# One token-row fetch a pass, VectorE in written order, and another order of passes and of last norms in a mixture-of-experts decoder layer

## The chip, the cores and the metric

One NeuronCore of a Trainium2 chip runs the whole layer. The metric is the device time of one execution in microseconds (us). A time is the median of three executions; the profile is of one more execution of the same program.

## The reference

The input is 512 tokens of 1024 float32 numbers. The layer projects them, runs four mLSTM heads and eight sliding-window attention heads side by side, adds the result to the input and normalises. Then comes a mixture of 32 experts, of which each token uses two, and a second normalisation:

```python
def hierarchical_moe(...):
    g_idx = argmax(xt @ w_group_router + b)          # one of 4 groups
    top_v, top_i = top_k(e_logits of that group, 2)  # two of its 8 experts
    ...
    for e in range(N_EXPERTS):                        # D_EXPERT = 256
        h = silu(xt @ w_exp_gate[e]) * (xt @ w_exp_up[e])
        out = out + combine[:, e:e + 1] * (h @ w_exp_down[e])
...
x = layer_norm(ALPHA * x + hierarchical_moe(x), ln2_w, ln2_b)
```

Everything that the change touches lies in the mixture of experts and in the last normalisation.

## The kernel before

**Passes.** Once the tokens have been routed, the kernel works in 13 passes, numbered p = 0 to 12. A pass holds 128 seats for tokens, shared out among experts by the letter that `ORDER` gives it: A is one expert with 96 seats and one with 32, B is two experts with 64 seats each, C is four experts with 32 seats each. An expert has 3 MB of weights, so an A or B pass needs 6 MB and a C pass 12 MB. In `"BBBCABABACBBC"` the C passes are 3, 9 and 12.

**What a pass does.** `pairs_x` (L1019) collects the tokens of two passes at a time by products of one-hot tiles (`ohr`, written by VectorE in `hot`, L1012 and L1014) with the token rows `x1h` and `x1l`; `pick_out` (L1025, L1027) copies the result to `xs`. `gu_part` (L1106) is gate and up, one half of the weights after the other; `pair_h` makes the hidden vector (ScalarE L1119, VectorE L1120); `dn_t` transposes it (TensorE L1127, VectorE copy to `ht`, L1129); `dn_mm` (L1137) is down. TensorE's order is written out: gate and up of pass p with the transpose of pass p-1 in its middle, then, for odd p, the collection of the next two passes, then down of pass p-1.

**What becomes of a pass's result.** For p below `KEPT` = 8, `y_store` writes the weighted rows to `yd` in HBM. For later passes `y_split` (L1147 on ScalarE, L1148 on VectorE) cuts them in two parts, `back_hot` (L1173, VectorE) writes a one-hot tile, and `add_back` adds them into the token rows `x1`: eight pairs of products on TensorE (L1185), each followed by a VectorE add (L1186), through two PSUM banks. For the stored rows, `y_gather` fetches each of the four chunks of 128 tokens twice by an indirect DMA on GpSimd's queue (memset L1162, DMA L1163) and VectorE adds them to `x1` (L1166). It is called in passes 8 (chunks 0 and 1) and 9 (chunks 2 and 3).

**Orders and queues.** SyncE's queue carries the weights in a written order (L596 gate and up, L602 and L604 down). They go into a ring of 16 slots of 1 MB (7 + 5 + 4); `release` gives back a pass's gate and up slots and the down slots of the pass before it, `prefetch` issues as many loads as slots have been given back, and each waits on the queue until the last reader of its slot is done. Activations share 16 slots of 4 KB a partition (`mix`): the eight tiles `x1h` and `x1l` hold half of them until the last collection; `xs`, `ohr`, `y`, `yh`, `yl`, `oh2` and `yg` share the rest. A block under `manual_schedule` keeps the written order on the engines that it names; the other engines' order comes from a planner with its own costs. In the pass loop only TensorE (and SyncE) were so named.

**The end.** After the loop a block with the four compute engines in written order does down of pass 11, its `add_back`, and pass 12. A token's final row is normalised by `norm_s` (statistics on VectorE L1618, a short chain on GpSimd), `norm_z` (ScalarE L1630, times `ln2_w` L1631) and `norm_o` (plus `ln2_b` L1636, DMA out L1637). Tokens that have a seat in pass 12 are normalised once more: `base_rows` (L1657, L1659) collects their rows into the PSUM tiles `zr`, the result of pass 12 is added there, and the rows are scattered out (L1707). In VectorE's written order the multiplication of pass 12's hidden vector (L1120) stands behind `norm_z` of chunk 3.

Of the kernel before, what the change touches and what calls it, by code (L numbers as in the profile page):

```python
# [10 lines left out]
F32 = mybir.dt.float32  # L11
F32R = mybir.dt.float32r
# [4 lines left out]
AF = mybir.ActivationFunctionType  # L17
OP = mybir.AluOpType
AX = mybir.AxisListType
ENG = mybir.EngineType  # L20

T = 512
DM = 1024
NCH = 4
P = 128
# [2 lines left out]
DE = 256  # L28
CAP = 64

ORDER = "BBBCABABACBBC"
NP = len(ORDER)
STATIC = 6
NOVER = 32
# [13 lines left out]
KEPT = 8  # L48
# [30 lines left out]
def layer_kernel(ctx, tc, x, w_in, conv_w, conv_b, gate_bias, norm_w, sinks, w_out, ln1_w, ln1_b,  # L79
# [20 lines left out]
    def slot(name, dt=F32, pool=None):  # L100
        _, p_, n = pools[pool or ("front" if name in FRONT else "mix")]
        return p_.tile([P, n], dt, tag="s", name=name)
# [85 lines left out]
    def split(hi, lo, src, eng=V):  # L188
        A.activation(hi, src, AF.Copy)  # L189
        eng.tensor_tensor(lo, src, hi, op=OP.subtract)  # L190
# [887 lines left out]
    def ready(p):  # L1078
        return fetch(p) if p in GATHER else hots(p)
# [75 lines left out]
        G.dma_start(yd[p * P:(p + 1) * P], y)  # L1155


    def y_gather(cs):
        for c in cs:
            for k in range(2):  # L1160
                t = slot("yg")[:, :DM]
                G.memset(t, 0.0)  # L1162
                G.indirect_dma_start(out=t, out_offset=None, in_=yd[:, :],  # L1163
                                     in_offset=bass.IndirectOffsetOnAxis(ap=yrow[:, 2 * c + k:2 * c + k + 1], axis=0),
                                     bounds_check=KEPT * P - 1, oob_is_err=False)
                V.tensor_add(x1[c], x1[c], t)  # L1166

    def y_slots():
        return [slot(n, F32R)[:, :DM] for n in ("yh", "yl")]
# [410 lines left out]
    def back(p):  # L1580
        return back_hot(slot("oh2", F32R)[:, 0:T], toks(p))

    with tc.manual_schedule(engines={ENG.PE}):
        for p in range(2, NP - 1):
            release(p, False)
            if p > 2:
                release(p - 1, True)
            prefetch(99)
            hts = []
            pg = pg2 if p == 2 else pass_gu(xs, p % 2, p, (lambda: hts.append(dn_t(prev))) if prev else None)  # L1590
            h = pair_h(pg)
            if p % 2:
                ob, xs = hn, taken(p + 1, hn)
                if p + 3 < NP:
                    hn = ready(p + 3)
            if prev:
                py = pass_dn(hts[0], p - 1)
                if p - 1 < KEPT:
                    y_store(py, p - 1)
                else:  # L1600
                    y = y_split(py, cws[:, p - 1:p], *y_slots())
                    if p == NP - 2:
                        ht = dn_t(h)
                    add_back(back(p - 1), y)
                if p - KEPT in (0, 1):
                    y_gather(range(2 * (p - KEPT), 2 * (p - KEPT) + 2))
            prev = h
        l2d = l2_parts()
        o = back(NP - 2)
        sm = same_rows(NP - 1)  # L1610

    HS = [slice(0, 512), slice(512, 1024)]
    mvs = {}
# [9 lines left out]

    zo = {}

    def norm_z(c):
        z = zo[c] = slot("z")[:, :DM]
        mv = mvs[c]
        for h, hs in enumerate(HS):
            A.activation(z[:, hs], x1[c][:, hs], AF.Identity, bias=mv[:, 3:4], scale=mv[:, 2:3])  # L1630
            (G if ('VV', 'VG', 'VV', 'GV')[c][h] == "G" else V).tensor_mul(z[:, hs], z[:, hs], l2[0][:, hs])  # L1631

    def norm_o(c):
        z = zo.pop(c)
        for h, hs in enumerate(HS):
            (G if ('VV', 'VV', 'GV', 'GV')[c][h] == "G" else V).tensor_add(z[:, hs], z[:, hs], l2[1][:, hs])  # L1636
        SP.dma_start(o2[c * P:(c + 1) * P], z)  # L1637

    def base(c):
        return [x1[c][:, hs] for hs in HS]  # L1640
# [3 lines left out]
    prefetch(99)  # L1644
    with tc.manual_schedule(engines=MAN):
        zr = [bank("zr", tag=t) for t in ("t", "m")]
        fin = {}

        def x1_fin(c):
            fin[c] = [slot(n, F32R)[:, :DM] for n in ("fh", "fl")]  # L1650
            split(*fin[c], x1[c], (G, None, None, None)[c])

        def base_rows(c):
            for h in range(2):
                if c in fin:
                    for s, t in enumerate(fin[c]):
                        TE.matmul(zr[h], ob[:, c, 0:P], t[:, HS[h]], start=c == 0 and s == 0, stop=False)  # L1657
                else:
                    TE.matmul(zr[h], ob[:, c, 0:P].bitcast(F32), x1[c][:, HS[h]], start=c == 0, stop=False)  # L1659

        def last_gu(u):
            for g in range(2):
                gu_part(pg, xs, 0, pairs[p], TILES[ORDER[p]], 2 * u + g)

        y = y_split(pass_dn(ht, p - 1), cws[:, p - 1:p], *y_slots())
        add_back(o, y, (0,))
        l2_fill(0)
        add_back(o, y, (1,))
        l2_fill(1)
        norm_s(0, base(0))  # L1670
        x1_fin(0)
        add_back(o, y, (2,))
        norm_z(0)
        add_back(o, y, (3,))
        pg = bank("pg")
        last_gu(0)
        norm_s(1, base(1))
        norm_o(0)
        norm_z(1)
        base_rows(0)  # L1680
        norm_s(2, base(2))
        base_rows(1)
        norm_o(1)
        norm_z(2)
        base_rows(2)
        norm_s(3, base(3))
        base_rows(3)
        norm_o(2)
        norm_z(3)
        last_gu(1)  # L1690
        h = pair_h(pg)
        ht = dn_t(h)
        norm_o(3)
        py = pass_dn(ht, p)
        held_y = slot("yf")[:, :DM]
        A.activation(held_y[:, HS[0]], py[0], AF.Copy, scale=cws[:, p:p + 1])
        V.tensor_scalar(held_y[:, HS[1]], py[1], cws[:, p:p + 1], None, op0=OP.mult)
        for h in range(2):
            TE.matmul(zr[h], sm, held_y[:, HS[h]], start=False, stop=True)
        norm_s(4, zr)  # L1700
        mv = mvs[4]
        z = slot("z")[:, :DM]
        for h, hs in enumerate(HS):
            V.scalar_tensor_tensor(z[:, hs], zr[h], mv[:, 0:1], l2[0][:, hs], op0=OP.subtract, op1=OP.mult)
        for h, hs in enumerate(HS):
            V.scalar_tensor_tensor(z[:, hs], z[:, hs], mv[:, 2:3], l2[1][:, hs], op0=OP.mult, op1=OP.add)
        G.indirect_dma_start(out=o2[:, :], out_offset=bass.IndirectOffsetOnAxis(ap=row[:, 0:1], axis=0),  # L1707
                             in_=z, in_offset=None, bounds_check=T - 1, oob_is_err=False)
# [28 lines left out]
    with tc.For_i(0, nmore, 1):  # L1737
        nx = nc.values_load(more[0:1, 0:1], min_val=0, max_val=NOVER // 2)
        with tc.For_i(0, nx, 1) as it:
            dyn_pair(it)  # L1740
        yh, yl = y_slots()
        split(yh, yl, held_y)
        add_back(back_hot(slot("oh2", F32R)[:, 0:T], toks(NP - 1)), (yh, yl))
        for c in range(NCH):
            norm_s(c, base(c))
            norm_z(c)
            norm_o(c)
    close_pool("ring2")
    close_pool("front")
    close_pool("ring1")  # L1750
# [46 lines left out]
```

## Time and profile before

| | |
|---|---|
| median of 3 executions | 561.29 us (555.67 to 566.44) |
| profiled execution, own time | 565.51 us |
| profiled execution, span | 563.8 us |
| TensorE busy | 501.7 us (89%) |
| VectorE busy | 282.8 us (50%) |
| ScalarE busy | 162.2 us (29%) |
| GpSimd busy | 154.8 us (27%) |
| read from HBM | 126.58 MB, 240 GB/s over the span |

The profiled execution's own time is 1.7 us over its span and 4.2 us over the median. Busy shares are averages over stages that have different limits, so the argument goes by stretches of the trace. PE is TensorE, DVE VectorE, ACT ScalarE, POOL GpSimd, SP SyncE; a float32 product shows as two records.

### The profile page before, as it was taken

What the parts mean: (1) busy time and instruction counts of PE and PEld (TensorE: products, weight loads), DVE (VectorE), ACT (ScalarE), POOL (GpSimd) and SP (SyncE); (2) the same over time, 40 slices, a digit from 0 to 9 for tenths busy, and PEclk for the clock granted to TensorE, in tenths of its full rate; (3) what the DMA queues carried; (4) which work ended last, traced back from release to release, by engine and by line L of the source; (5) the groups of instructions that cost most, each with busy time, mean ns of one, the idle gap of its engine ahead of it and who ended that gap; (6) DMA issues with size and microseconds to landing.
All of it is one profiled execution on the core that took longest, in us unless ns stands there. A gap on an engine that the chain in (4) does not pass through costs nothing. (4 is left out here: it accounts for less than half of the span.)

```text
span 563.8 us, 8436 instructions
## 1 busy us (share of the span) xinstructions
PE 501.7 (89%) x3048; PEld 337.6 (60%) x3048; DVE 282.8 (50%) x635; ACT 162.2 (29%) x351; POOL 154.8 (27%) x179
## 2 busy tenths in 40 slices
PE   6999899999999999798999999979955876998951
PEld 6998688788989878587355625426213522544310
DVE  3542877964487755988733311203003544246743
ACT  3452475774542513333111111111100100013210
POOL 5389715302211105567200000000330220010431
PEclk9999989999999999986999999999997896997877
DMA  8644203214935562965599999999999999950110
GB/s 238 177 113 113 76 2 111 76 40 140 415 99 168 188 175 99 341 235 245 180 372 380 370 409 391 415 412 402 402 421 420 420 421 357 347 183 0 75 76 19
DMA packets 44462, 134.20 MB, mean 238 GB/s; under 512 B 6718, under 2 KB 17998, under 8 KB 41088
## 3 DMA queue, kind: packets, MB, share of 16 engines
q1 hardware_dynamic: 41504, 126.04, 60.9%
q0 software_dynamic: 2912, 7.58, 3.7%
q8 instruction: 25, 0.41, 0.3%
q14 instruction: 21, 0.17, 0.1%
HBM read 126.58 MB, written 8.91 MB: 240 GB/s over the span
## 5 line engine op out<-in xcount | busy, mean ns | idle before, releaser
L1106 PE MATMUL pg<-we,xs 128*32 128x512 f32 (+1 forms) x608 | 105.5, 611 | 11.5 <-DMA we<-in_w_exp_up 11.4
L1106 PEld LDWEIGHTS pg<-we,xs 128*32 128x32 f32 (+1 forms) x608 | 28.1, 122 | 74.6 <-issue 71.4
L1019 PE MATMUL xp<-ohr,x1h 128*128 128x256 f32 (+1 forms) x224 | 58.4, 299 | 7.5 <-DVE ht L1129 5.7
L244 PE MATMUL pj<-wh,xh 128*128 128x256 f32 (+1 forms) x224 | 63.6, 286 | 1.1 <-ACT wh L189 1.1
L245 PE MATMUL pj<-wh,xl 128*128 128x256 f32 (+1 forms) x224 | 62.8, 282 | 0.1
L1137 PE MATMUL yo<-we,ht 128*32 128x512 f32 (+1 forms) x304 | 54.1, 671 | 8.0 <-DVE ht L1129 8.0
L1019 PE MATMUL xp<-ohr,x1l 128*128 128x256 f32 (+1 forms) x224 | 56.9, 293 | 0.0
L1019 PEld LDWEIGHTS xp<-ohr,x1h 128*128 128x128 f32 x224 | 45.7, 204 | 13.2 <-DVE ht L1129 5.9
L249 PE MATMUL pj<-wl,xh 128*128 128x256 f32 x192 | 52.5, 279 | 0.0
L1019 PEld LDWEIGHTS xp<-ohr,x1l 128*128 128x128 f32 x224 | 45.4, 203 | 0.0
L244 PEld LDWEIGHTS pj<-wh,xh 128*128 128x128 f32 x224 | 42.4, 189 | 1.3 <-ACT wh L189 1.3
L245 PEld LDWEIGHTS pj<-wh,xl 128*128 128x128 f32 x224 | 42.4, 189 | 0.3 <-DVE xl L190 0.3
L1155 POOL DMA_DIRECT2D yd<-y x8 | 4.4, 551 | 129.1 <-ACT y L1154 120.5
L1119 ACT ACTIVATE hid<-pg 128x256 f32<-128x256 f32 x13 | 5.0, 382 | 119.2 <-PE pg L1106 119.2
L1137 PEld LDWEIGHTS yo<-we,ht 128*32 128x32 f32 (+1 forms) x304 | 15.0, 131 | 39.0 <-issue 27.5
L1129 DVE COPY ht<-ph 128x256 f32<-128x256 f32 x13 | 5.5, 423 | 60.7 <-PE ph L1127 60.7
L249 PEld LDWEIGHTS pj<-wl,xh 128*128 128x128 f32 x192 | 35.6, 188 | 0.0
L190 DVE TENSOR_TENSOR wl<-wraw,wh 128x1024 fp32r<-128x1024 f32 x14 | 20.3, 1464 | 23.8 <-ACT wh L189 23.7
L1166 DVE TENSOR_TENSOR x<-x,yg 128x1024 f32<-128x1024 f32 x8 | 9.8, 1224 | 35.8 <-DMA yg<-yd,yrow 35.8
L189 ACT ACTIVATE wh<-wraw 128x1024 fp32r<-128x1024 f32 (+2 forms) x23 | 23.2, 1021 | 12.4 <-PE pj L245 4.1
L193 PE MATMUL pj<-xh,wh 128*128 128x512 f32 x64 | 26.7, 416 | 0.0
L195 PE MATMUL pj<-xl,wh 128*128 128x512 f32 x64 | 26.6, 416 | 0.0
(359 smaller groups left out, 987.4 us busy)
## 6 DMA issues: line engine op xcount, KB each, us to landing
we<-in_w_exp_gate SPq DMA_DIRECT2D x64, 512.0 KB, 11.6
we<-in_w_exp_up SPq DMA_DIRECT2D x64, 512.0 KB, 11.9
we<-in_w_exp_down SPq DMA_DIRECT2D x26, 1024.0 KB, 12.9
wraw<-in_w_in SPq DMA_DIRECT2D x20, 512.0 KB, 3.6
we<-in_w_exp_down SPq DMA_DIRECT2D x12, 512.0 KB, 7.1
yd<-y POOLq DMA_DIRECT2D x8, 512.0 KB, 7.6
xc<-in_x SPq DMA_DIRECT2D x4, 512.0 KB, 9.6
wo<-in_w_out SPq DMA_DIRECT2D x8, 256.0 KB, 4.4
```

The lines of the kernel that those rows point to most:

```text
L189: A.activation(hi, src, AF.Copy)
L190: eng.tensor_tensor(lo, src, hi, op=OP.subtract)
L193: TE.matmul(o, lh, rh, start=start, stop=False)
L195: TE.matmul(o, lh, rl, start=False, stop=stop)
L244: TE.matmul(o, xh[j // 2][:, j % 2, cs], ws[i][j][0], start=j == 0, stop=False)
L245: TE.matmul(o, xl[j // 2][:, j % 2, cs], ws[i][j][0], start=False, stop=False)
L249: TE.matmul(o, xh[k // 2][:, k % 2, cs], ws[i][k][1], start=False, stop=k == 7)
L1019: TE.matmul(p_[:, j2, 0:P * n], w[c][:, 2 * g + j2], o[:, c, 0:P * n], start=c == 0 and s == 0 and j2 == 0, stop=c == NCH - 1 and s == 1 a ...
L1106: TE.matmul(pg[s:s + n], xs[k // 4][:, k % 4, P * b + s:P * b + s + n], ws[e][k // 4][:, :, k % 4], start=k == 0, stop=k == 7)
L1129: V.tensor_copy(ht, ph)
L1137: TE.matmul(py[u][s:s + n], ht[:, j, s:s + n], wt[e][2][j][:, 512 * u:512 * u + 512], start=j == 0, stop=j == 1)
L1166: V.tensor_add(x1[c], x1[c], t)
```

## The change

- `ORDER` becomes `"BBBCABABABBCC"`: the four-expert passes are 3, 11 and 12, and pass 9 is a B.
- `y_gather` is cut into `y_fetch` (memset and indirect DMA of one chunk) and `y_add` (its two VectorE adds). Chunks 0, 1 and 2 are fetched at the end of passes 8, 9 and 10 and added at the end of passes 9, 10 and 11, behind `add_back`; chunk 3 is fetched in pass 11 behind the collection for pass 12, and added after the loop.
- The pass loop's block names VectorE too, so VectorE keeps the written order there.
- `l2_parts` (which prepares `ln2_w` and `ln2_b` for a broadcast) moves into pass 11, and `l2_fill` (TensorE L1561, ScalarE copies L1563) from between the pieces of the last `add_back` to the end of the loop's block.
- At the end, all norms of the four chunks stand before pass 12 in VectorE's order, staggered over the chunks; three additions of `ln2_b` go to GpSimd; the DMAs out are issued after all of them. `base_rows` takes chunk 0 as float32 like the others: the split of `x1[0]` into `fh` and `fl` is gone. TensorE's order at the end is `add_back`, first half of gate and up, all `base_rows`, second half.

```diff
-ORDER = "BBBCABABACBBC"
+ORDER = "BBBCABABABBCC"
...
-    def y_gather(cs):
-        for c in cs:
-            for k in range(2):
-                t = slot("yg")[:, :DM]
-                G.memset(t, 0.0)
-                G.indirect_dma_start(out=t, ...)
-                V.tensor_add(x1[c], x1[c], t)
+    def y_fetch(c):
+        ts = [slot("yg")[:, :DM] for _ in range(2)]
+        for k, t in enumerate(ts):
+            G.memset(t, 0.0)
+            G.indirect_dma_start(out=t, ...)
+        return c, ts
+
+    def y_add(c, ts):
+        for t in ts:
+            V.tensor_add(x1[c], x1[c], t)
...
-    with tc.manual_schedule(engines={ENG.PE}):
+    with tc.manual_schedule(engines={ENG.PE, ENG.DVE}):
         for p in range(2, NP - 1):
...
                 ob, xs = hn, taken(p + 1, hn)
                 if p + 3 < NP:
                     hn = ready(p + 3)
+            if p == NP - 2:
+                l2d = l2_parts()
+                yg3 = y_fetch(NCH - 1)
             if prev:
                 py = pass_dn(hts[0], p - 1)
...
                     add_back(back(p - 1), y)
-                if p - KEPT in (0, 1):
-                    y_gather(range(2 * (p - KEPT), 2 * (p - KEPT) + 2))
+                if p > KEPT:
+                    y_add(*yg)
+                if KEPT <= p < NP - 2:
+                    yg = y_fetch(p - KEPT)
             prev = h
-        l2d = l2_parts()
+        y_add(*yg3)
         o = back(NP - 2)
         sm = same_rows(NP - 1)
+        for i in range(2):
+            l2_fill(i)
...
         y = y_split(pass_dn(ht, p - 1), cws[:, p - 1:p], *y_slots())
-        add_back(o, y, (0,))
-        l2_fill(0)
-        add_back(o, y, (1,))
-        l2_fill(1)
+        add_back(o, y, (0, 1))
         norm_s(0, base(0))
-        x1_fin(0)
         add_back(o, y, (2,))
+        norm_i(0)
+        norm_s(1, base(1))
+        add_back(o, y, (3,))
+        norm_i(1)
         norm_z(0)
-        add_back(o, y, (3,))
+        norm_s(2, base(2))
+        norm_o(0, 0, G)
+        norm_z(1)
+        norm_i(2)
+        norm_s(3, base(3))
+        norm_o(1, 0, G)
+        norm_o(0, 1, V)
+        norm_z(2)
+        norm_i(3)
+        norm_o(2, 0, G)
+        norm_o(1, 1, V)
+        norm_z(3)
+        norm_o(2, 1, V)
+        norm_o(3, 0, V)
+        norm_o(3, 1, V)
+        for c in range(NCH):
+            norm_d(c)
         pg = bank("pg")
         last_gu(0)
-        norm_s(1, base(1))
-        norm_o(0)
-        norm_z(1)
-        base_rows(0)
-        norm_s(2, base(2))
-        base_rows(1)
-        norm_o(1)
-        norm_z(2)
-        base_rows(2)
-        norm_s(3, base(3))
-        base_rows(3)
-        norm_o(2)
-        norm_z(3)
+        for c in range(NCH):
+            base_rows(c)
         last_gu(1)
         h = pair_h(pg)
         ht = dn_t(h)
-        norm_o(3)
         py = pass_dn(ht, p)
```

Here `norm_i` is the ScalarE part of the old `norm_z`, `norm_z` the multiplication by `ln2_w`, `norm_o(c, h, engine)` the addition of one half of `ln2_b`, and `norm_d` the DMA out.

## Rows read from the trace of the kernel before

**Rows 1.** The page's part with the span in 40 slices of 14.1 us each: busy tenths of TensorE, the clock granted to it in tenths of full speed, the busy share of the DMA engines, and what they moved.

```profile
PE   6999899999999999798999999979955876998951
PEclk9999989999999999986999999999997896997877
DMA  8644203214935562965599999999999999950110
GB/s 238 177 113 113 76 2 111 76 40 140 415 99 168 188 175 99 341 235 245 180 372 380 370 409 391 415 412 402 402 421 420 420 421 357 347 183 0 75 76 19
```

**Rows 2.** Whom TensorE waited for between 400 and 564 us: us in total, times, longest.

```profile
PE yo L1137 <- DVE ht L1129: 8.0, 3, 6.8
PE pg L1106 <- DMA we<-in_w_exp_up: 7.7, 5, 2.2
PE xp L1019 <- DVE ht L1129: 5.7, 1, 5.7
PE ph L1127 <- DVE hid L1120: 5.3, 1, 5.3
```

**Rows 3.** Whom VectorE waited for in the same stretch.

```profile
DVE x L1166 <- DMA yg<-yd,yrow: 35.8, 6, 21.1
```

**Rows 4.** TensorE's timeline in gate and up of pass 9, which is a C before: start, duration, and in brackets the idle time before the first of a row and what ended it.

```profile
405.37 1.05 PE L1106 MATMUL pg<-we,xs 128*32 128x512 f32 x4
...
410.02 4.75 PE L1106 MATMUL pg<-we,xs 128*32 128x512 f32 x28 [1.43 <-DMA we<-in_w_exp_up]
...
421.97 2.74 PE L1106 MATMUL pg<-we,xs 128*32 128x512 f32 x10 [2.19 <-DMA we<-in_w_exp_up]
```

**Rows 5.** TensorE's timeline at two collections (L1019) and the down step behind each: that of pass 7, and that of pass 9.

```profile
383.00 0.39 PE L1019 MATMUL xp<-ohr,x1h 128*128 128x256 f32 x1
...
390.77 3.64 PE L1137 MATMUL yo<-we,ht 128*32 128x512 f32 x32
...
427.58 0.38 PE L1019 MATMUL xp<-ohr,x1h 128*128 128x256 f32 x1
...
435.44 0.58 PE L1019 MATMUL xp<-ohr,x1h 128*128 128x256 f32 x1 [5.72 <-DVE ht L1129]
...
443.30 3.64 PE L1137 MATMUL yo<-we,ht 128*32 128x512 f32 x32
```

**Rows 6.** TensorE's timeline from gate and up of pass 10 (a B) over down of pass 9 to gate and up of pass 11.

```profile
453.87 5.37 PE L1106 MATMUL pg<-we,xs 128*64 128x512 f32 x24
...
459.61 1.94 PE L1106 MATMUL pg<-we,xs 128*64 128x512 f32 x8
468.39 6.42 PE L1137 MATMUL yo<-we,ht 128*32 128x512 f32 x32 [6.85 <-DVE ht L1129]
...
481.64 5.37 PE L1106 MATMUL pg<-we,xs 128*64 128x512 f32 x24
```

**Rows 7.** TensorE's timeline at the end: the transpose behind down of pass 10, the first product of the last `add_back`, then gate and up, `base_rows`, gate and up, and down of pass 12.

```profile
500.12 0.51 PE L1127 MATMUL ph<-ident,hid 128*128 128x128 f32 x2
...
511.12 0.47 PE L1185 MATMUL cb<-yh,oh 128*128 128x512 f32 x1 [0.19 <-DVE x L1186]
...
523.46 4.50 PE L1106 MATMUL pg<-we,xs 128*32 128x512 f32 x32
...
528.93 5.31 PE L1659 MATMUL zr<-x,ohr 128*128 128x512 f32 x12
534.17 3.64 PE L1106 MATMUL pg<-we,xs 128*32 128x512 f32 x32
...
544.29 6.02 PE L1137 MATMUL yo<-we,ht 128*32 128x512 f32 x32 [0.52 <-DVE ht L1129]
```

**Rows 8.** VectorE's timeline: the first and the last add of a fetched chunk, a multiplication by `ln2_w` at the end, and pass 12's hidden vector.

```profile
423.86 1.23 DVE L1166 TENSOR_TENSOR x<-x,yg 128x1024 f32<-128x1024 f32 x1 [21.07 <-DMA yg<-yd,yrow]
...
466.78 1.23 DVE L1166 TENSOR_TENSOR x<-x,yg 128x1024 f32<-128x1024 f32 x1 [1.83 <-DMA yg<-yd,yrow]
...
522.17 2.54 DVE L1631 TENSOR_TENSOR z<-z,l 128x512 f32<-128x512 f32 x2
...
542.61 0.41 DVE L1120 TENSOR_TENSOR hid<-hid,pg 128x256 f32<-128x256 f32 x1
```

**Rows 9.** VectorE's groups between 380 and 564 us: count, busy us in total, mean ns of one, idle time before.

```profile
L1186 DVE TENSOR_TENSOR x<-x,cb 128x512 f32<-128x512 f32 x32 | 20.8, 684 | 7.5 <-PE cb L1185 7.5
L1166 DVE TENSOR_TENSOR x<-x,yg 128x1024 f32<-128x1024 f32 x8 | 9.8, 1224 | 35.8 <-DMA yg<-yd,yrow 35.8
...
L1618 DVE BATCH_NORM_STATS2 lnst<-x 128x6 f32<-128x512 f32 x8 | 5.1, 679 | 0.0
L1636 DVE TENSOR_TENSOR z<-z,l 128x512 f32<-128x512 f32 x6 | 3.8, 660 | 0.0
L1014 DVE SCALAR_TENSOR_TENSOR ohr<-iot,pcol,ohr 128x256 fp32r<-128x256 f32 x8 | 3.6, 476 | 0.0
...
L1173 DVE TENSOR_SCALAR oh<-iot,tok 128x256 fp32r<-128x256 f32 x8 | 3.0, 389 | 0.0
```

**Rows 10.** GpSimd's timeline: the memset of the last two fetched tiles.

```profile
453.77 1.84 POOL L1162 MEMSET yg<- 128x1024 f32 x2 [6.94 <-PE cb L1185]
```

**Rows 11.** SyncE's queue: the issue of the 80th megabyte of weights, and how long the transfers issued between 440.3 and 442.5 us took to land.

```profile
441.56 0.33 SPq L596 DMA_DIRECT2D we<-in_w_exp_up  x1
DMA to landing us min/median/max: 14.3/14.4/14.5
```

More of the change, by code (lines that the diff above doesn't have):

```diff
@@ L1155, in y_store @@
         G.dma_start(yd[p * P:(p + 1) * P], y)
-    def y_gather(cs):
-        for c in cs:
-            for k in range(2):
-                t = slot("yg")[:, :DM]
-                G.memset(t, 0.0)
-                G.indirect_dma_start(out=t, out_offset=None, in_=yd[:, :],
-                                     in_offset=bass.IndirectOffsetOnAxis(ap=yrow[:, 2 * c + k:2 * c + k + 1], axis=0),
-                                     bounds_check=KEPT * P - 1, oob_is_err=False)
-                V.tensor_add(x1[c], x1[c], t)
+    def y_fetch(c):
+        ts = [slot("yg")[:, :DM] for _ in range(2)]
+        for k, t in enumerate(ts):
+            G.memset(t, 0.0)
+            G.indirect_dma_start(out=t, out_offset=None, in_=yd[:, :],
+                                 in_offset=bass.IndirectOffsetOnAxis(ap=yrow[:, 2 * c + k:2 * c + k + 1], axis=0),
+                                 bounds_check=KEPT * P - 1, oob_is_err=False)
+        return c, ts
+    def y_add(c, ts):
+        for t in ts:
+            V.tensor_add(x1[c], x1[c], t)
     def y_slots():
@@ L1624, in layer_kernel, with norm_i, norm_o, norm_d @@
     zo = {}
-    def norm_z(c):
[L1627 to L1637, printed above, removed]
+    def norm_i(c):
+        z, mv = slot("z")[:, :DM], mvs[c]
+        zo[c] = z
+        for hs in HS:
+            A.activation(z[:, hs], x1[c][:, hs], AF.Identity, bias=mv[:, 3:4], scale=mv[:, 2:3])
+    def norm_z(c):
+        for hs in HS:
+            V.tensor_mul(zo[c][:, hs], zo[c][:, hs], l2[0][:, hs])
+    def norm_o(c, h, eng):
+        eng.tensor_add(zo[c][:, HS[h]], zo[c][:, HS[h]], l2[1][:, HS[h]])
+    def norm_d(c):
+        SP.dma_start(o2[c * P:(c + 1) * P], zo.pop(c))
     def base(c):
@@ L1646, in layer_kernel @@
         zr = [bank("zr", tag=t) for t in ("t", "m")]
[L1647 to L1651, printed above, removed]
         def base_rows(c):
             for h in range(2):
[L1655 to L1659, printed above, removed]
+                TE.matmul(zr[h], ob[:, c, 0:P].bitcast(F32), x1[c][:, HS[h]], start=c == 0, stop=False)
         def last_gu(u):
@@ L1745, in layer_kernel @@
             norm_s(c, base(c))
+            norm_i(c)
             norm_z(c)
-            norm_o(c)
+            for h in range(2):
+                norm_o(c, h, V)
+            norm_d(c)
     close_pool("ring2")
```

## The prediction

> **What bounds the kernel now.** I read the slices first. From about 280 us the DMA engines are full at some 400 GB/s and stay so, with one dip, until about 500 us; then there are 64 us with almost no transfer, in the first three slices of which TensorE is still 80% busy or more, and its granted clock drops in places [rows 1]. So the weights alone do not set the end: what runs after the last weight has landed does. The question is why so much is left by then. Next I read whom TensorE waits for after 400 us [rows 2]: weights for 7.7 us, and VectorE (`ht`, in three places, and `hid`) for some 19 us. The wait for weights lies in gate and up of pass 9, a four-expert pass [rows 4]; up to there TensorE follows the weights, and behind it nothing on TensorE waits for weights any more. Why VectorE is late is told by its own waits: 35.8 us for the fetched rows of `yd` [rows 3], one of 21 us alone [rows 8]. The adds of fetched rows stand ahead of `ht` in its queue; TensorE stops 5.72 us in the collection [rows 5] and 6.85 us before down of pass 9 [rows 6]. From pass 9 on the chain is therefore TensorE, held up by VectorE, to the end. Each of its stops before the last pass is worth its length, as long as the weights do not become the bound instead.
>
> **The four-expert pass goes from 9 to 11.** Pass 9 takes TensorE from 405.37 to 427.58, 22.2 us [rows 4, 5]. A B pass without waits takes 453.87 to 461.55, 7.7 us [rows 6]. Pass 9 as a B needs the megabytes 61 to 64 in the order of the queue; the last of these is what the fourth expert of the C pass waited for, there at 410.02 [rows 4]. TensorE would want it after half its work, at 409.2, so it waits 0.8 us and ends at 413.9: **13.7 us earlier**.
>
> In return pass 11 is a C, and its gate and up need megabytes 73 to 80. The queue moves the same bytes, and only which experts come first is changed, so I take the landing of the trace: the 80th is issued at 441.56 and lands 14.4 us later, at 456.0 [rows 11]. Below, TensorE comes to pass 11 at 453.0 and to its second half at 456.9. That is just covered. If the cover is gone, each microsecond by which the 80th is late costs one. The last four megabytes land by about 500 [rows 1], and down of pass 12 will want them after 510. The ring of 16 slots does not hold the loads back: the slots for megabytes 87 to 94 come back from pass 11's own gate and up, the first four by 457, while in steady flow the 87th would be issued at about 460.
>
> **VectorE in written order, fetches a pass earlier than their adds.** The adds of chunk 0 now stand behind `add_back` of pass 8, and the fetch is done long before (first rows there at 423.86 [rows 8], the add at about 434). A fetch took 13.0 us from its memset at 453.77 [rows 10] to the last add at 466.78 [rows 8]; between fetch and add there now lies a pass of gate and up, down and `add_back`, some 18 us (7.7 + 3.6 + 6.8, the last from the end of down of pass 9 at 474.81 to 481.64 [rows 6]). So both stops go. In the collection behind pass 9, TensorE takes 427.58 to 443.30, 15.7 us, against 383.00 to 390.77, 7.8 us, for the same work without a stop [rows 5]: **7.9 us**, of which 5.7 are the stop and the rest a clock that fell in it. Before down of pass 9 it is 6.85 us of stop and 6.42 us for what took 3.64 us elsewhere [rows 5, 6]: **9.6 us**.
>
> What the written order adds: eight one-hot fills (L1012, L1014) now stand ahead of `y_split` instead of between the copies, and both fills of `oh` behind it. The fills are some 3.3 us (8 x 0.476 is an upper bound of 3.8), the `oh` pair 0.8 us [rows 9]. Down of the pass before (3.64 us) covers the first; the second stands in front of `add_back`. Bounds are 0 and 4.6 us a pass; I take 1.3 us, near the uncovered `oh` pair plus the overhang, for two passes: **2.6 us back**. TensorE then starts pass 11 at 481.64 - 13.7 - 7.9 - 9.6 + 2.6 = 453.0, and ends down of pass 10 at 500.12 - 28.6 = 471.5 [rows 6, 7].
>
> **From there to the hidden vector of pass 12.** Before, this is 500.12 to 542.61, 42.5 us [rows 7, 8]. First part, to the start of the last `add_back`: 11.0 us before (511.12 [rows 7]). Now four adds of fetched rows (chunks 2 and 3, 4 x 1.22 = 4.9 us [rows 9]) stand on VectorE between the two `add_back`s, and `l2_fill` on TensorE; I count 8.7 us to the end of `add_back` of pass 10 (6.8 as behind down of pass 9, 1.3 for the written order, 0.6 for the last add), 4.9 for the adds and 3.0 for the small steps behind them, so 16.6 us: **5.6 us back**. Chunk 3's fetch starts when the collection for pass 12 frees the eight tiles of `x1h` and `x1l`, at about 468.5; with 13.0 us it is there at 481.5, and VectorE wants it at 482.6. This is as tight as pass 11's weights.
>
> Second part, 31.5 us before, with VectorE and TensorE waiting for each other in turns. Now TensorE: about 8.4 us of `add_back` in VectorE's pace (eight adds of 0.684, four statistics of 0.679 between them), 4.1 us for half of gate and up (between 3.64 and 4.50 [rows 7]), 16 records of `base_rows` at 5.31/12 = 0.44 us, 7.1 us, 3.6 us for the other half, 0.6 us of ScalarE: 23.8 us. VectorE beside it: eight adds 5.5, eight statistics 5.4, eight multiplications 5.3 and five additions 3.3 us [rows 9], 19.5 us and some 1.4 for small ones, 20.9 us. So TensorE ends it and the part is **7.5 us shorter**.
>
> A row speaks against that sum: two multiplications that take 1.32 us took 2.54 us beside a GpSimd subtraction [rows 8, 9]. The Trainium skill (SBUF — State Buffer, Who interferes with whom) says that a VectorE instruction with two SBUF inputs and a GpSimd instruction that reads SBUF shut each other out for a whole instruction, and by it the three additions that go to GpSimd here would be no gain for VectorE. The trace agrees in that row. By the row each GpSimd addition may cost VectorE up to 1.2 us, so VectorE's sum is 20.9 to 24.5 us against TensorE's 23.8: at most 0.7 us, kept in the range.
>
> **From the hidden vector to the end.** Before, 563.8 - 542.6 = 21.2 us. Down of pass 12 took 6.02 us at the lower clock [rows 7], after 5.3 us in which TensorE waited for `hid` [rows 2]. That wait is now about 1.2 us, and down took 3.64 us after shorter gaps [rows 5]: **2.4 us less**; bounds 0 and 2.4, the short gap being nearer to the second.
>
> **Sum.** -13.7 - 7.9 - 9.6 + 2.6 + 5.6 - 7.5 - 2.4 = -32.9 us: span 530.9, own time 532.6 against 565.51. The median of the runs shown is 561.29, 0.9925 of that; scaled the same way 528.6. I predict 529 us, 0.94 of the time before. About 2% is what a measurement of this kernel can tell from no change: 550.1 to 572.5.
>
> **Rivals.**
> - *The tail gets no shorter*: all norms still stand ahead of pass 12's hidden vector in VectorE's order, and chunk 3's fetch stands ahead of them. If the chains through GpSimd and ScalarE are not hidden (the 7.5 us) or the fetch is late by as much, the span is 538.5, the median 536. For it: the tight 481.5 against 482.6. Against it: the norms are staggered by two chunks.
> - *The wait for weights only moves*: two C passes in a row need 24 MB through 16 slots. If megabytes 77 to 80 are late by the 13.7 us that pass 9 waited, the span is 544.6, the median 542. Against it: the landing at 456.0 [rows 11].
> - *The written order takes the stops along*: `mix` has 16 tiles, and when `y_split` of pass 8 is written I count all of them taken (eight of `x1h` and `x1l`, two `xs`, one `ohr`, `yh`, `yl`, `oh2`, two `yg`). So a fetch can start only when tiles of the pass before are freed; a memset has waited 6.94 us for `add_back` in this way [rows 10]. If the planner gives the tiles only behind the next `add_back`, VectorE stands for the whole fetch, 13.0 us, with `ht`, the hidden vector and the next `add_back` behind it, and the down step behind runs 2.8 us slower [rows 5, 6]. One such stop is 15.8 us. Two give a span of 562.5, median 560: no change, the edit not doing what it says. All three (chunks 1, 2, 3) give 578.3, median 575.6: **slower than before**. It is slower at all from 11 us a stop on, and by over 2% from about 15. Against it: nothing else is on GpSimd's queue in these passes.
>
> **How the numbers follow.** Forecast 0.53, with a range of its own of 522 to 536 (no cost of the written order and the fetched adds half hidden below; no gain of clock, 0.7 us of port and 4 us of late weights above). Tail no shorter 0.16, weights 0.12, two stops 0.09, three stops 0.06, better than 522 0.04. The range 521 to 544 leaves out the stops and the case below. Faster by over 2%: 0.53 + 0.16 + 0.12 + 0.04 = 0.85; within 2% 0.09; slower 0.06.
>
> **What would show it.** Right: gate and up of pass 9 in some 8.5 us; collection and down steps at 7.8 and 3.64 us with no wait for `ht`; VectorE's wait for fetched rows (35.8 us) near nothing; gate and up of pass 12 starting near 496 instead of 523.46; the wait for `hid` near 1 us. Wrong: TensorE waiting for weights in pass 11 by over 4 us, VectorE standing at its adds of fetched rows, or a last `add_back` that starts much later than 16.6 us after down of pass 10.

## The result and the profile after

The changed kernel takes **534.86 us** (median of four executions, 529.61 to 535.69), 0.953 of the time before [0.942, 0.964]: faster by over 2%. Its profiled execution has a span of 532.4 us and an own time of 534.1 us. I had said 529 us, a span of 530.9 and a range of 521 to 544. The ratios here and below are taken from a kernel's faster executions alone, and two profiles of slower ones (end alone; `oh` first) are not read for their stretches.

The page's slices, now 13.3 us each:

```profile
PE   6999899999999999978899999899897988988881
...
PEclk9999999999999999989799999999999978989896
DMA  8724212221974538287569999999999999999030
GB/s 230 209 83 121 76 41 84 75 80 51 372 250 119 196 122 248 62 333 254 222 207 370 372 369 415 388 421 408 398 412 422 422 417 422 419 420 379 15 158 20
```

Transfers now run without a dip to some 490 us, and what TensorE does behind the last weight takes some 40 us instead of the 64 of [rows 1]. Whom TensorE waited for between 380 us and the end: us in total, times, longest.

```profile
PE cb L1188 <- DVE oh L1176: 6.2, 3, 2.2
PE pg L1106 <- DMA we<-in_w_exp_up: 3.4, 2, 2.5
PE cb L1188 <- DVE yl L1148: 1.7, 1, 1.7
PE cb L1188 <- DVE x L1189: 1.7, 3, 1.3
PE ph L1127 <- DVE hid L1120: 1.0, 1, 1.0
PE yo L1137 <- DVE ht L1129: 0.5, 1, 0.5
```

Against [rows 2] the waits for `ht` fell from 13.7 us to 0.5 and that for `hid` from 5.3 to 1.0. A new wait stands first, for the one-hot tile `oh`, three times. VectorE's wait for fetched rows, 35.8 us in [rows 3], is in no row any more; its group of those adds now reads (busy, mean ns, idle before):

```profile
L1169 DVE TENSOR_TENSOR x<-x,yg 128x1024 f32<-128x1024 f32 x8 | 9.7, 1222 | 0.1
```

TensorE's timeline of the same places as [rows 4 to 7]: gate and up of pass 9, the collection, down of pass 8 with its `add_back`, the starts of passes 10 and 11, the transpose behind down of pass 10, the last `add_back`, and pass 12.

```profile
401.21 1.02 PE L1106 MATMUL pg<-we,xs 128*64 128x512 f32 x2
403.17 3.65 PE L1106 MATMUL pg<-we,xs 128*64 128x512 f32 x16 [0.93 <-DMA we<-in_w_exp_up]
409.28 1.90 PE L1106 MATMUL pg<-we,xs 128*64 128x512 f32 x6 [2.46 <-DMA we<-in_w_exp_up]
...
413.41 0.39 PE L1019 MATMUL xp<-ohr,x1h 128*128 128x256 f32 x1
...
421.23 3.64 PE L1137 MATMUL yo<-we,ht 128*32 128x512 f32 x32
427.10 0.48 PE L1188 MATMUL cb<-yh,oh 128*128 128x512 f32 x1 [2.23 <-DVE oh L1176]
...
428.66 0.79 PE L1188 MATMUL cb<-yh,oh 128*128 128x512 f32 x1 [0.25 <-DVE x L1189]
...
434.81 5.37 PE L1106 MATMUL pg<-we,xs 128*64 128x512 f32 x24
...
454.37 5.36 PE L1106 MATMUL pg<-we,xs 128*32 128x512 f32 x48
...
472.83 0.50 PE L1127 MATMUL ph<-ident,hid 128*128 128x128 f32 x2
...
488.07 0.47 PE L1188 MATMUL cb<-yh,oh 128*128 128x512 f32 x1
...
502.10 7.13 PE L1663 MATMUL zr<-x,ohr 128*128 128x512 f32 x16
...
513.79 0.51 PE L1127 MATMUL ph<-ident,hid 128*128 128x128 f32 x2 [0.99 <-DVE hid L1120]
514.81 3.64 PE L1137 MATMUL yo<-we,ht 128*32 128x512 f32 x32 [0.52 <-DVE ht L1129]
```

VectorE's timeline: `yl`, `oh`, two places with fetched rows, a multiplication by `ln2_w`, and pass 12's hidden vector.

```profile
425.29 1.40 DVE L1148 SCALAR_TENSOR_TENSOR yl<-yo,cws,yh 128x512 fp32r<-128x512 f32 x2
426.61 0.60 DVE L1176 TENSOR_SCALAR oh<-iot,tok 128x256 fp32r<-128x256 f32 x2
...
435.52 2.48 DVE L1169 TENSOR_TENSOR x<-x,yg 128x1024 f32<-128x1024 f32 x2
...
482.79 4.87 DVE L1169 TENSOR_TENSOR x<-x,yg 128x1024 f32<-128x1024 f32 x4
...
508.10 2.60 DVE L1644 TENSOR_TENSOR z<-z,l 128x512 f32<-128x512 f32 x2 [1.01 <-ACT z L1640]
...
513.31 0.42 DVE L1120 TENSOR_TENSOR hid<-hid,pg 128x256 f32<-128x256 f32 x1 [0.81 <-ACT hid L1119]
```

GpSimd's timeline: the memsets of chunks 1, 2 and 3, the last indirect fetch of chunk 3, and two additions of `ln2_b`.

```profile
434.52 1.84 POOL L1161 MEMSET yg<- 128x1024 f32 x2 [20.27 <-PE cb L1188]
...
454.27 1.84 POOL L1161 MEMSET yg<- 128x1024 f32 x2 [15.36 <-PE cb L1188]
...
472.14 1.83 POOL L1161 MEMSET yg<- 128x1024 f32 x2
...
475.47 1.00 POOL L1162 DMA_INDIRECT yg<-yd,yrow  x1 [0.30 <-issue]
...
507.18 2.96 POOL L1647 TENSOR_TENSOR z<-z,l 128x512 f32<-128x512 f32 x2
```

Cut at the same places, the two traces give the gain, and beside it what I had put there (us; minus is faster):

| stretch | before | after | difference | forecast |
|---|---|---|---|---|
| start to gate and up of pass 9 | 405.37 | 401.21 | -4.2 | 0 |
| gate and up of pass 9 | 22.21 | 12.20 | -10.0 | -13.7 |
| collection | 15.72 | 7.82 | -7.9 | -7.9 |
| down of pass 8 to pass 10 | 10.57 | 13.58 | +3.0 | +1.3 |
| pass 10 to pass 11 | 27.77 | 19.56 | -8.2 | -8.3 |
| pass 11 to the end of down of pass 10 | 18.48 | 18.46 | 0.0 | 0 |
| to the last `add_back` | 11.00 | 15.24 | +4.2 | +5.6 |
| to pass 12's hidden vector | 31.49 | 25.24 | -6.3 | -7.5 |
| to the end | 21.2 | 19.1 | -2.1 | -2.4 |
| sum | 563.8 | 532.4 | -31.4 | -32.9 |

These are two single executions; between the medians the difference is 26.4 us.

### The profile page after: what moved, and what is told of

It is laid out like the page before. It is cut to its first block, busy times and chain, and to the rows that moved or that the text cites. A ratio compares the mean times of both kernels' runs of the same rounds, so it can differ in the third digit from the quotient of the medians.

```text
span 532.4 us, 8435 instructions
## 1 busy us (share of the span) xinstructions
PE 485.1 (91%) x3048; PEld 331.4 (62%) x3048; DVE 284.6 (53%) x636; ACT 161.3 (30%) x350; POOL 152.2 (29%) x177
## 5 line engine op out<-in xcount | busy, mean ns | idle before, releaser
L1106 PE MATMUL pg<-we,xs 128*32 128x512 f32 (+1 forms) x608 | 98.9, 604 | 7.4 <-DMA we<-in_w_exp_up 7.4
L1019 PE MATMUL xp<-ohr,x1h 128*128 128x256 f32 (+1 forms) x224 | 57.0, 295 | 1.7 <-DVE ohr L1014 1.7
L1019 PE MATMUL xp<-ohr,x1l 128*128 128x256 f32 (+1 forms) x224 | 55.7, 289 | 0.0
L1019 PEld LDWEIGHTS xp<-ohr,x1h 128*128 128x128 f32 x224 | 44.5, 199 | 7.4 <-issue 4.9
L1137 PE MATMUL yo<-we,ht 128*32 128x512 f32 (+1 forms) x304 | 47.4, 595 | 0.5 <-DVE ht L1129 0.5
L1019 PEld LDWEIGHTS xp<-ohr,x1l 128*128 128x128 f32 x224 | 44.4, 198 | 0.0
L190 DVE TENSOR_TENSOR wl<-wraw,wh 128x1024 fp32r<-128x1024 f32 x14 | 20.4, 1466 | 23.8 <-ACT wh L189 23.7
L1025 DVE COPY xs<-xp 128x512 f32<-128x512 f32 (+1 forms) x12 | 7.8, 647 | 38.1 <-PE xp L1019 38.1
L1188 PE MATMUL cb<-yh,oh 128*128 128x512 f32 x32 | 18.6, 580 | 8.4 <-DVE oh L1176 6.2
```

Of the source, the lines that this page charges most:

```text
L1019: TE.matmul(p_[:, j2, 0:P * n], w[c][:, 2 * g + j2], o[:, c, 0:P * n], start=c == 0 and s == 0 and j2 == 0, stop=c == NCH - 1 and s == 1 a ...
L1025: V.tensor_copy(d, p_[:, :, 0:P * n])
L1106: TE.matmul(pg[s:s + n], xs[k // 4][:, k % 4, P * b + s:P * b + s + n], ws[e][k // 4][:, :, k % 4], start=k == 0, stop=k == 7)
L1137: TE.matmul(py[u][s:s + n], ht[:, j, s:s + n], wt[e][2][j][:, 512 * u:512 * u + 512], start=j == 0, stop=j == 1)
L1188: TE.matmul(b, o[:, c * P:(c + 1) * P], t[:, us], start=i == 0, stop=i == 1)
```

## The experiments

Two theories stood against each other. The first is the forecast: the three parts are separate terms, each stop on TensorE being worth its length. The second: the parts need one another, since a stop that ends with a landing only grows when TensorE comes to it earlier. The front of the kernel, which the change leaves alone, varies: gate and up of pass 1 begins at 269.5 to 275.1 us. The medians are from several chips, so rows are compared by their ratios, each to executions of the kernel before on the same chip, and besides by the stretch of the profile from pass 1 to the end. A second profile of the changed kernel (the repeat below) gave 258.6 us for it against 261.9; a difference under some 3.3 us in that column is not told from a repeat.

| kernel | median us | ratio to the kernel before | from pass 1 to the end, us |
|---|---|---|---|
| before | 561.29 | | 290.5 |
| order alone | 554.01 | 0.991 [0.986, 0.996] | 281.9 |
| loop alone | 563.11 | 1.005 [0.9995, 1.010] | 286.1 |
| end alone | 554.22 | 0.988 [0.976, 0.999] | not read |
| changed, old order | 551.01 | 0.980 [0.969, 0.991] | 275.7 |
| changed, old end | 544.85 | 0.972 [0.964, 0.979] | 271.0 |
| changed, fetch and add in one pass | 545.39 | 0.973 [0.967, 0.980] | 271.6 |
| changed, planner for VectorE | 530.53 | 0.946 [0.941, 0.951] | 255.4 |
| changed, `oh` first, hidden vector first | 529.37 | 0.935 [0.927, 0.944] | not read |
| changed, C passes 10 to 12 | 537.69 | 0.961 [0.957, 0.966] | 261.7 |
| planner, hidden vector first | 528.91 | 0.942 [0.935, 0.949] | 254.2 |
| the same, silu ahead of the last norm | 528.22 | 0.943 [0.940, 0.945] | 254.3 |
| changed, once more, beside the last | 537.36 | 0.960 [0.956, 0.964] | 258.6 |

**Order alone.** In the kernel before:

```diff
-ORDER = "BBBCABABACBBC"
+ORDER = "BBBCABABABBCC"
```

> The kernel before with the new order of passes alone. My theory (TensorE is the chain from pass 9 on, and its waits are worth their length): gate and up of pass 9 falls from 22.2 to some 8.5 us, the two stops for VectorE (5.7 and 6.9 us) stay, and the time falls by the 13.7 us of that term, to about 548 us. Rival (the wait for weights only moves): TensorE waits some 14 us for weights in gate and up of pass 11, and the time stays at 558 to 562 us.

Measured 0.991, some 5 us where I had expected 13.7. Pass 9's gate and up ended at 414.89 instead of 427.58, 12.7 us earlier (1.7 of them from an earlier start of pass 1), against the 13.7 of the sum. TensorE's timeline then shows the stop in the collection and the first product of the `add_back` of pass 9, and VectorE's shows adds of fetched rows:

```profile
432.05 0.58 PE L1019 MATMUL xp<-ohr,x1h 128*128 128x256 f32 x1 [15.02 <-DVE ht L1129]
...
464.77 0.47 PE L1185 MATMUL cb<-yh,oh 128*128 128x512 f32 x1 [3.22 <-DVE oh L1173]
```

```profile
421.90 1.22 DVE L1166 TENSOR_TENSOR x<-x,yg 128x1024 f32<-128x1024 f32 x1 [21.64 <-DMA yg<-yd,yrow]
...
430.43 1.23 DVE L1166 TENSOR_TENSOR x<-x,yg 128x1024 f32<-128x1024 f32 x1 [1.77 <-DMA yg<-yd,yrow]
```

The stop in the collection is 15.02 us long, against 5.72 in [rows 5]: the rows land when they land (421.9, against 423.9 in [rows 8]), TensorE is only there sooner. 9.3 of the 12.7 us went into the longer wait. The second theory held here. I had expected both stops to stay as they were; the second one, before down of pass 9, was gone instead. In the planner's order `ht` now stood ahead of chunk 3's last add, and TensorE waited 3.22 us for `oh` in place of 6.85 for `ht`: from pass 10 to pass 11 it took 21.26 us against 27.77. Those 6.5 us are most of what the order gave alone.

**Loop alone.** `y_fetch` and `y_add`, VectorE named in the loop, chunk 3 in pass 11; the order of passes and the end as before:

```diff
-    with tc.manual_schedule(engines={ENG.PE}):
+    with tc.manual_schedule(engines={ENG.PE, ENG.DVE}):
...
-                if p - KEPT in (0, 1):
-                    y_gather(range(2 * (p - KEPT), 2 * (p - KEPT) + 2))
+                if p > KEPT:
+                    y_add(*yg)
+                if KEPT <= p < NP - 2:
+                    yg = y_fetch(p - KEPT)
```

> The kernel before with the loop's part alone: one chunk fetched a pass and added a pass later, VectorE in written order; the old order of passes and the old end. My theory: both stops go (7.9 and 9.6 us with the clock), the written order costs 2.6 us, and the adds of chunks 2 and 3 now lie ahead of the last add_back (5.6 us): 9.3 us less, about 552 us. Rival (the written order takes the stops along, or the adds moved to the end cost what the stops did): 560 us or more.

No gain by the ratio, 1.005, where I had expected 552 us (the profile has 4.4 us less from pass 1): the rival came. TensorE's timeline at gate and up of pass 11, the transpose behind down of pass 10, and the last `add_back`:

```profile
471.79 5.37 PE L1106 MATMUL pg<-we,xs 128*64 128x512 f32 x24
...
490.27 0.51 PE L1127 MATMUL ph<-ident,hid 128*128 128x128 f32 x2
...
508.77 0.76 PE L1188 MATMUL cb<-yh,oh 128*128 128x512 f32 x1 [6.69 <-DVE oh L1176]
```

Both stops are gone and pass 11 begins 9.9 us earlier than in [rows 6]. From the transpose to the last `add_back` there are then 18.5 us instead of 11.0 [rows 7], 6.7 of them a wait for `oh`, which stands behind the four adds on VectorE: the work left the stops and most of it came back at the end. The changed kernel needs 15.2 us there.

**End alone.** The new order of the norms and `l2_fill` at the end of the loop (`l2_parts` stays behind the loop):

```diff
-        add_back(o, y, (0,))
-        l2_fill(0)
-        add_back(o, y, (1,))
-        l2_fill(1)
+        add_back(o, y, (0, 1))
         norm_s(0, base(0))
-        x1_fin(0)
...
```

> The kernel before with the end's part alone: staggered norms ahead of pass 12's hidden vector, base_rows of chunk 0 as float32, l2_fill at the end of the loop's block. My theory: 7.5 us from the first product of the last add_back to the hidden vector and 2.4 us in down of pass 12, so about 551 us. Rival (the norms are only moved from one place of VectorE's queue to another): 558 to 562 us, with the wait of TensorE for the hidden vector still near 5 us.

0.988 [0.976, 0.999]: some 7 us against the 9.9 expected, which lies within the interval. By their ratios the three parts alone give -0.9, +0.5 and -1.2%, together -1.7%; the whole change gives -4.7% (-4.0% in the repeat).

**The whole without one part.** First the old `ORDER` in the changed kernel:

```diff
-ORDER = "BBBCABABABBCC"
+ORDER = "BBBCABABACBBC"
```

> The changed kernel with the old order of passes (four-expert pass at 9 again). My theory: the 13.7 us of pass 9 come back, about 548 us. Rival (with the stops gone, the weights set the pace, and where the four-expert pass lies is the same to the time): 533 to 538 us.

The stretch from pass 1 is 13.8 us longer than after (17.1 than its repeat); TensorE waits 8.6 us for weights in pass 9 again. On top of the other parts the order is worth at least the 13.7 us of the sum; alone, by the same column, 8.6. Next, the end of the kernel before in the changed one:

```diff
-        add_back(o, y, (0, 1))
+        add_back(o, y, (0,))
+        l2_fill(0)
+        add_back(o, y, (1,))
+        l2_fill(1)
         norm_s(0, base(0))
+        x1_fin(0)
...
```

> The changed kernel with the old end (norms between the pieces of pass 12, chunk 0 of base_rows split, l2_fill between the pieces of the last add_back). My theory: the end is worth 7.5 + 2.4 us also on top of the rest, so about 545 us, with TensorE waiting some 5 to 6 us for the hidden vector of pass 12 again. Rival (the end's gain is only shown where the loop runs late, as for the order and the loop alone, which gave less alone than together): 535 to 538 us.

9.1 us longer than after (12.4 than its repeat); the sum had 9.9 for the end (7.5 and 2.4). Its TensorE rows are those of the kernel before, the wait for `hid` and the slow down of pass 12:

```profile
519.77 0.70 PE L1127 MATMUL ph<-ident,hid 128*128 128x128 f32 x2 [5.16 <-DVE hid L1120]
520.98 6.13 PE L1137 MATMUL yo<-we,ht 128*32 128x512 f32 x32 [0.52 <-DVE ht L1129]
```

This kernel is also the order alone with the loop's part added, and so says what the loop is worth behind the new order: 281.9 less 271.0, 10.9 us, against 4.4 in the kernel before. Order and loop together give 19.5 us, alone 8.6 and 4.4. The loop takes away the stop that the order alone only lengthens.

**Is it the pass between, or the written order?** First the distance of a pass is taken away for chunks 0 to 2:

```diff
-                if p > KEPT:
-                    y_add(*yg)
                 if KEPT <= p < NP - 2:
-                    yg = y_fetch(p - KEPT)
+                    y_add(*y_fetch(p - KEPT))
```

> The changed kernel with the adds of chunks 0, 1 and 2 right behind their fetch, in the same pass, in VectorE's written order. My theory (a stop lasts until the rows land, some 13 us from the memset, and TensorE stands for what ht and the next add_back come later): three stops in passes 8, 9 and 10 of 5 to 15 us each on TensorE, 20 to 40 us in all, so 555 to 575 us. Rival (stops ahead of pass 11 cost little, since TensorE would meet the weights there): at most 545 us.

It costs 9.7 us in the column (13.0 against the repeat; 0.973), fewer than I expected. VectorE's wait (total, times, longest), then where it stops TensorE:

```profile
DVE x L1169 <- DMA yg<-yd,yrow: 23.6, 3, 22.3
```

```profile
427.46 0.58 PE L1019 MATMUL xp<-ohr,x1h 128*128 128x256 f32 x1 [7.39 <-DVE ht L1129]
```

Only chunk 0 stops. Its fetch begins after the rows of pass 7 are stored (store issued at 405.24, fetch at 415.52). Chunks 1 and 2 are there within a pass even so: GpSimd's order is the planner's, their fetches went out early in the pass (the last at 437.25 and 453.49), and VectorE came to the adds at 448.55 and 468.11 without a wait. Then the distance is kept and the planner gets VectorE back:

```diff
-    with tc.manual_schedule(engines={ENG.PE, ENG.DVE}):
+    with tc.manual_schedule(engines={ENG.PE}):
```

> The changed kernel with VectorE's order in the loop left to the planner again; fetches and adds stay a pass apart in the text. If the distance between fetch and add is what matters: VectorE's wait for fetched rows stays under 5 us and the time at 530 to 538 us. If the written order matters: the planner puts the adds ahead of ht once more, VectorE waits over 10 us for fetched rows, and the time is 542 us or more.

No wait for fetched rows appears, and the stretch from pass 1 is 255.4, 3.2 to 6.5 us less than in the two profiles of the changed kernel. (The interval of its ratio overlaps that of the first measurement of the changed kernel and not that of its repeat.) So with the pass between fetch and add no stop is left, whoever orders VectorE, and the written order gains nothing that shows and probably costs something. Of the stops, the distance is shown to remove chunk 0's; whether one chunk a pass alone would remove the others, with the planner and without the distance, was not run. VectorE and TensorE between down of pass 8 and its `add_back`:

```profile
427.24 0.75 DVE L1148 SCALAR_TENSOR_TENSOR yl<-yo,cws,yh 128x512 fp32r<-128x512 f32 x1 [2.38 <-ACT yh L1147]
427.91 0.34 DVE L1176 TENSOR_SCALAR oh<-iot,tok 128x256 fp32r<-128x256 f32 x1
```

```profile
428.40 0.48 PE L1188 MATMUL cb<-yh,oh 128*128 128x512 f32 x1 [1.09 <-DVE oh L1176]
...
434.37 5.37 PE L1106 MATMUL pg<-we,xs 128*64 128x512 f32 x24
```

The planner writes the first half of `oh` between the halves of `yl`; in written order both halves of `yl` come first (425.29 and 426.61 above). TensorE waits 1.09 us here instead of 2.23, and 3.8 instead of 6.2 in all three places.

**Are the weights the next bound?** The C passes last:

```diff
-ORDER = "BBBCABABABBCC"
+ORDER = "BBBABABABBCCC"
```

> The changed kernel with all three four-expert passes last (10, 11 and 12 instead of 3, 11 and 12). My theory: TensorE is set free from the weights in passes 4 to 9, but meets them in gate and up of passes 10 and 11, whose weights cannot land sooner; passes 11 and 12 need the same megabytes of the queue as now, so the time stays at 531 to 536 us, with a wait for weights in pass 11 of what TensorE came earlier. Rival (each four-expert pass that moves behind the others gives some 13 us, as the one from 9 to 11 did): 518 to 524 us.

537.7 us (I had said 531 to 536), 261.7 from pass 1: no gain. TensorE in pass 11:

```profile
447.07 3.39 PE L1106 MATMUL pg<-we,xs 128*32 128x512 f32 x27
...
456.44 1.88 PE L1106 MATMUL pg<-we,xs 128*32 128x512 f32 x2 [2.71 <-DMA we<-in_w_exp_up]
```

It begins pass 11 at 447.07 instead of 454.37, waits 5.0 us for weights in it and runs part of it at the lower clock (0.50 to 0.55 granted from 456.4 to 463.0). The collection behind it begins 190.6 us after the start of pass 1, in the two profiles of the changed kernel 191.5 and 189.2. What came early was lost again in pass 11: up to there the weights are the bound right behind.

**Towards a faster version.** First both orders around `oh` and `hid`: `oh` written ahead of the collection, and half of pass 12's gate and up before the last `add_back`, its hidden vector before the norm of chunk 3:

```diff
+            if p > KEPT:
+                obk = back(p - 1)
             if p % 2:
                 ob, xs = hn, taken(p + 1, hn)
...
-                    add_back(back(p - 1), y)
+                    add_back(obk, y)
...
+        pg = bank("pg")
+        last_gu(0)
         add_back(o, y, (0, 1))
...
         norm_o(1, 1, V)
+        for c in range(NCH):
+            base_rows(c)
+        last_gu(1)
+        h = pair_h(pg)
+        ht = dn_t(h)
         norm_z(3)
```

> The changed kernel with two edits at places where TensorE still waits: the one-hot tile oh of add_back is written ahead of the collection (TensorE waited 6.2 us for it in three places), and the first half of pass 12's gate and up goes ahead of the last add_back, where TensorE stands for VectorE, with the norm of chunk 3 behind pass 12's hidden vector on VectorE. My theory (TensorE and VectorE are the chain, weights are not): 2 to 3 us and 3 to 5 us less, 527 to 530 us. Rival (the weights of passes 11 and 12 are the bound by now): TensorE waits for weights instead, and the time stays at 533 to 537 us.

529.37 us, 0.935 [0.927, 0.944], as expected. Then the planner for VectorE with the edit of the end alone (the last two pieces of that diff):

> The changed kernel with VectorE's order in the loop left to the planner, and the first half of pass 12's gate and up ahead of the last add_back, with the norm of chunk 3 behind pass 12's hidden vector. My theory: the gains of the two add up, 530.5 less 3 us, 526 to 529 us, below both kernels. Rival (the end is set by VectorE's norms, so that TensorE's half of gate and up only moves a wait): 530 to 533 us, with TensorE's wait for the hidden vector longer than 2 us.

528.91 us, in the range that I gave, but that the two gains add up is not shown: from pass 1 it is 1.2 us less than the planner's version, and the ratios' intervals overlap. The rival's sign came too: TensorE at pass 12 waits over 2 us, since silu for `hid` now stands behind `norm_i(3)` on ScalarE:

```profile
507.19 0.51 PE L1127 MATMUL ph<-ident,hid 128*128 128x128 f32 x2 [2.09 <-DVE hid L1120]
508.21 5.34 PE L1137 MATMUL yo<-we,ht 128*32 128x512 f32 x32 [0.52 <-DVE ht L1129]
```

So `norm_i(3)` goes behind it:

```diff
-        norm_i(3)
         norm_o(2, 0, G)
...
         ht = dn_t(h)
+        norm_i(3)
         norm_z(3)
```

> As the kernel with the planner's loop and pass 12's first half moved up, but on ScalarE the last normalising step of chunk 3 now stands behind pass 12's silu instead of ahead of it (there it waited for GpSimd 2.2 us, and silu behind it, and the down step that followed 2.1 us of TensorE's waiting took 5.34 us instead of 3.64). My theory: the wait for the hidden vector falls to 1 us, down takes 3.64 us, 2 to 3 us less than 528.9, about 526 us. Rival (VectorE or GpSimd ends the last stretch anyway): 528 to 530 us.

> The changed kernel itself once more, on the chip of the run beside it, so that the two can be held against the same runs of the kernel before: 0.95 of the kernel before, 533 to 536 us.

TensorE at down of pass 11 and at pass 12, in the new version:

```profile
482.94 4.92 PE L1137 MATMUL yo<-we,ht 128*32 128x512 f32 x32
...
509.58 0.51 PE L1127 MATMUL ph<-ident,hid 128*128 128x128 f32 x2 [0.98 <-DVE hid L1120]
510.61 3.64 PE L1137 MATMUL yo<-we,ht 128*32 128x512 f32 x32 [0.52 <-DVE ht L1129]
```

The gap and the slow down step of pass 12 are gone, as expected, and from its transpose to the end it takes 18.3 us instead of 20.0. The time did not follow (528.22, where I had expected 526, and 254.3 against 254.2 from pass 1): down of pass 11 took 4.92 us here with no wait ahead of it, and 1.0 us was lost before pass 10. On one chip this version takes 528.22 us and the changed kernel 537.36, and the intervals of their ratios do not touch. It beats both kernels. The changed kernel's repeat lies 1.4 us above what I had given for it.

## Why the prediction was right, point by point

**Right.** The bound was read rightly: pass 9 following the weights, then TensorE held up by VectorE to the end. Pass 9 ended at 413.41 (413.9 in the sum). It took 12.2 us instead of the 8.5 that I had named as a sign: TensorE came to it 4.2 us earlier than in the trace before, 2.8 of which arose before pass 1, and spent the lead waiting 3.4 us for weights. The collection took 7.82 us. Pass 11 began at 454.37 (453.0) and did not wait for weights, so the landing read from [rows 11] was enough, and the rival with the weights fell. The last `add_back` began at 488.07, where the terms put 471.5 + 16.6 = 488.1. That this agrees so well is luck: down of pass 10 was 1.3 us late, and the parts of the 16.6 (8.7, 4.9 and 3.0) were 10.0, 4.9 and 0.4, since most of the small steps came behind the first product, as a wait of 1.7 us for `yl`. The wait for `hid` was 0.99 us and the last down step 3.64. The rival with the unshortened end fell at 25.2 us against 31.5.

**The rival with 16 tiles** had its premise right: the memsets of chunks 1 and 2 stood 20.27 and 15.36 us until `add_back` gave tiles back. But the tiles came back with the `add_back` that stands ahead of the fetch in the text, not the next one, and a whole pass was left for the fetch, so its consequence did not come. Chunk 3, with a memset at 472.14 instead of the 468.5 I took, was the closest. The four adds from 482.79 on are chunk 2's two and then chunk 3's, whose first began at about 485.2; by my 13.0 us its rows were due at 485.1. VectorE did not wait: the two fetches, the last issued at 475.47, landed 8.0 to 8.7 us after their issue.

**Sizes that were off.** The written order: I took 1.3 us a pass. Between down of pass 8 and pass 10 it was +3.0 (+2.2 in the repeat): the 2.23 us for `oh` and an `add_back` at a lower clock behind it. In the two passes of the term the planner's version takes 10.7 and 18.0 us, the changed kernel 13.6 and 19.6 (12.8 and 18.8 in the repeat), so the written order cost 2.9 to 4.5 us against my 2.6 (the bounds had 0 to 4.6 a pass). The second part of the end took 25.2 instead of 24.0 us; the last `add_back` took 9.4 us of it, where the sum had 8.4. (Eight adds and four statistics by [rows 9] are 8.2, and by the sum's own 23.8 us the part would be 7.7 us shorter, not 7.5.) Nor was all of GpSimd's work there new: of the last norm, two multiplications and two additions ran on GpSimd before the change; now VectorE has all eight multiplications and GpSimd three additions.

**The median.** My span was 1.5 us short, but the median 5.9. The rest is the step from own time to median: I scaled by 0.9925, since the profiled execution before was 4.2 us over its median; the new one (534.1) was 0.8 under. One profile's distance from its median did not carry over.

**Wrong, though the sum held.** "Each of its stops before the last pass is worth its length" is no rule that adds: with the loop as before, 9.3 us of the order's 12.7 vanished in a longer first stop, and the second stop, priced at 9.6, was mostly gone without the loop's part; in the kernel before with the loop's part alone, 7.5 of the 9.9 us came back between down of pass 10 and the last `add_back`. The sum came out because all the parts are there at once. And I put the removed stops under "VectorE in written order, fetches a pass earlier than their adds"; the written order was not needed for it. What the loop is worth behind the order and the new end together was not run; as a remainder it is 28.6 - 13.8 - 9.1 = 5.7 us, and 2.4 by the repeat. Why the front varies by some 5 us between runs stays open.

## What to carry to other kernels

Mark for each stop what ends it: one that ends with a landing can grow by what is gained ahead of it (5.7 us became 15.0 here), so take its cause away first and only then count the gains ahead of it. Distance from its use did more for a fetch here than a place in a written order; after moving it, look for the small tile (`oh` here) that now stands behind it on the same engine. A planner can do as well as a written order for one engine, or better, even where another's is written out.

## What the runs showed of the hardware

**TensorE's clock behind short gaps.** After the 2.23 us wait for `oh`, the `add_back` of pass 8 ran in part at the lower of TensorE's two levels (1.2 GHz): the granted clock between 427.1 and 434.8 us was 0.56, and records that take 0.39 to 0.50 us took 0.63 to 0.80. The length of the gap does not settle it. Behind waits of 1.07 to 1.09 us for `oh` the clock stayed at 1.00, in the kernel before and in two versions with the planner. Behind waits of some 2 us it differed from run to run of the same program: the three `add_back`s behind 2.23, 1.95 and 2.07 us had 0.56, 0.74 and 0.74 in the first profile of the changed kernel, and 0.75, 1.00 and 1.00 in the repeat. The three stretches that hold them took 48.4 and 45.9 us, which is most of the 3.3 us between the two profiles. Likewise the last down step, always with another gap of 0.52 us ahead of it: 3.64 us behind 0.99 and behind 1.68 (planner), 5.34 behind 1.66 (fetch and add in one pass) and 2.09, 6.02 behind 5.3 [rows 2, 7]. And in the last version down of pass 11 took 4.92 us at a granted clock of 0.73 with no wait ahead of it.

**VectorE beside GpSimd.** Two multiplications took 2.60 us (at 508.10) while GpSimd made two additions (2.96 us from 507.18); alone, two instructions of that shape take 1.32 by the mean of 660 ns in [rows 9]. In the kernel before, the two that took 2.54 us from 522.17 [rows 8] stood beside this row of GpSimd:

```profile
521.18 2.37 POOL L190 TENSOR_TENSOR fl<-x,fh 128x1024 fp32r<-128x1024 f32 x1
```

The Trainium skill (SBUF — State Buffer, Who interferes with whom) says that a VectorE instruction with two SBUF inputs contends with a GpSimd instruction that reads SBUF. Both traces agree. It cost nothing here: `hid` waited for ScalarE behind it.

**Transfers.** Between 420 and 480 us one core's queues moved 420 GB/s, and the six indirect fetches in it, each for 128 rows of 4 KB at most, landed 8.0 us (median) after their issue, with the engines full of weights.
